# Sums of squares for RMS norms: elementwise adds replaced by matmuls with a block of ones

## The chip, the cores and the metric

One core of a Trainium2 chip runs the whole program. The metric is device time in microseconds; before the change the median of three runs is 2202.68 us (2202.24 to 2213.45). TensorE does the matmuls, VectorE, ScalarE and GpSimd the elementwise work, and SyncE issues the DMAs.

## The reference

Two layers (shared shapes, own weights) run over 128 context tokens and 512 latent tokens, with a model width of 1024. Each layer has a mixer (two kinds of attention and two kinds of state-space scan, concatenated to 1024 features) and a gated convolutional FFN of inner width 2816. Around both stand RMS norms, and these are what the change is about:

```python
def rmsnorm(x, g):
    xf = x.astype(F32)
    y = xf * lax.rsqrt(jnp.mean(xf * xf, axis=-1, keepdims=True) + EPS)
    return (y * g.astype(F32)).astype(x.dtype)

# in each layer
    h = rmsnorm(x, P['g_pre1']) * (1.0 + scale1) + shift1        # then the mixer on h
    y = concat(ya, yb, yc, yd) @ P['w_out']
    x = x + gate1 * rmsnorm(y, P['g_post1'])
    h = rmsnorm(x, P['g_pre2']) * (1.0 + scale2) + shift2        # then the FFN on h
    x = x + gate2 * rmsnorm((jax.nn.silu(g) * v) @ P['w_down'], P['g_post2'])
```

So after each projection two sums of squares over 1024 features are needed per token: one of the projection's output `y`, then one of the new residual `x`, for the next block's norm.

## The kernel before

**Layout.** Features lie on the 128 partitions, in 8 chunks; tokens lie along the free dimension, 642 columns (512 latent, 2 empty, 128 context). The columns are worked in two halves, `SPANS`: 0 to 256 and 256 to 642 (386 columns), called `gi` 0 and 1. Linear layers split each float32 operand into a high and a low part in fp32r and take three products (`lin3`, L116), so that a chunk of 128 x 128 weights costs three matmuls a half.

**A norm.** A sum over features is a sum over 8 chunks and over 128 partitions. `sums` (L297) gives a PSUM tile and a dictionary; `square` (L301) squares a chunk on ScalarE (L309) and adds it to one of two running tiles, even chunks on VectorE and odd ones on GpSimd (L320), then merges the two (L322, L317). `rstd` (L324) sums over partitions: a matmul with 128 tokens of the running tile as weights and one column of ones, 2 token blocks in the first half, 3 in the second, there over two tiles (the eighth chunk's square is left apart). `spread` (L335) scales it and adds EPS on VectorE (L292), raises it to the power -0.5 on GpSimd (L294) and broadcasts it over the partitions by a matmul with the identity. `postnorm` (L381) multiplies `y` by it (L391, VectorE), adds it to `x` (L394, VectorE for even, GpSimd for odd chunks) and squares the new `x`; `prenorm` (L361) makes the next block's input `h` (L371 to L379).

**Buffers.** The first two squares of a sum have tiles of their own (`na00`, `na01`, `na10`, `na11`); all others come from the ring `nsr`, two buffers.

**Order.** Engines work their queues in order. The order in a queue is planned when the program is built, by a planner that simulates the engines and takes ready instructions by priority, which is mostly the order of the code; `prio` sets another. After attention, `run` (L1635 to L1642) goes: output projection of the first half with a square of each chunk (`put`), `norms` of the first half (its residual squares), then the projection of the second half. The prenorm of the first half is held as `pending` and called by `between` when the seventh projection chunk of the second half (`MID` = 6) is issued. The norms of the second half follow, and `ffn_first` starts the FFN's first eight up-projection tiles, of the first half, while these run. After the FFN of layer 0 the same `norms` runs beside the last down-projection (L1453 to L1466), and the first input projections of layer 1 start.

**At the start.** `rstd_first` (L346) already sums the squares of the input in another way: the square of chunk c is the moving operand of a matmul whose weights are 32 columns of ones, into partitions 32 (c mod 4) to +32 of one PSUM tile, two chunks into each. A ScalarE copy brings the tile to SBUF, and a matmul with `sel4` (ones in partitions 0, 32, 64, 96) adds the four rows. There the ring `nsr` has four buffers.

Of the kernel before, what the change touches and what calls it, by code (L numbers as in the profile page):

```python
# [8 lines left out]
F32 = mybir.dt.float32  # L9
F32R = mybir.dt.float32r  # L10
I32 = mybir.dt.int32
AF = mybir.ActivationFunctionType
# [3 lines left out]
P = 128  # L16
# [56 lines left out]
class K:  # L73
# [220 lines left out]
        self.nc.gpsimd.tensor_tensor(y, x, self.c("mhalf")[:, 0:n], op=ALU.pow)  # L294
        return y

    def sums(self, bank):  # L297

        return self.pss(bank), {}

    def square(self, pool, st, gi, src, c, n=8, tmp=None):  # L301


        t0, t1 = SPANS[gi]
        nc = self.nc
        first = n == 8 and c < 2
        tmp = (f"na{gi}{c}", t1 - t0, 1) if first else tmp or NTMP[gi]
        sq = pool.tile([P, tmp[1]], F32, tag=tmp[0], name="nsq", bufs=tmp[2])[:, :t1 - t0]
        nc.scalar.activation(sq, src[:, t0:t1], AF.Square)  # L309
        if first or n < 8:  # L310
            st[1][c] = sq
            return
        if c == 7:
            if gi == 1:
                st[1][c] = sq
            else:
                nc.vector.tensor_add(st[1][0], st[1][0], sq)  # L317
            return
        a = st[1][c % 2]
        (nc.gpsimd if c % 2 else nc.vector).tensor_add(a, a, sq)  # L320
        if c == 6:
            nc.vector.tensor_add(a, a, st[1].pop(1))  # L322

    def rstd(self, pool, st, gi, feats, tag="n"):  # L324

        t0, t1 = SPANS[gi]
        ps, sq = st[0], list(st[1].values())
        n = len(LOC[gi])
        for j, c in enumerate(LOC[gi]):
            for i, t in enumerate(sq):  # L330
                self.mm(ps[:, 400 + j:401 + j], t[:, c - t0:c - t0 + 128], self.c("ones")[:, 0:1], i == 0,
                        i == len(sq) - 1)
        return self.spread(pool, ps, gi, feats, tag)
# [11 lines left out]

    def rstd_first(self, pool, gi, bank):  # L346

        t0, t1 = SPANS[gi]
        ps = self.pss(bank)
        for c in range(8):  # L350
            sq = pool.tile([P, TW - SPLIT], F32, tag="nsr", name="nsq", bufs=4)[:, :t1 - t0]
            self.nc.scalar.activation(sq, self.x[c][:, t0:t1], AF.Square)
            j = c % 4
            self.mm(ps[32 * j:32 * j + 32, 0:t1 - t0], self.c("ones")[:, 0:32], sq, c < 4, c >= 4)
        sb = pool.tile([P, TW - SPLIT], F32, tag="nsr", name="nsb", bufs=4)
        self.nc.scalar.copy(sb[:, 0:t1 - t0], ps[:, 0:t1 - t0])
        for j, c in enumerate(LOC[gi]):
            self.mm(ps[:, 400 + j:401 + j], sb[:, c - t0:c - t0 + 128], self.c("sel4"), True, True)
        return self.spread(pool, ps, gi, 1024, "n")

    def prenorm(self, pool, l, which, gi, r):  # L361

# [38 lines left out]
    def norms(self, pool, gi, st, y, post, pre, out=None):  # L401


        nacc = self.sums("ud"[gi])
        if gi == 1:
            self.between(MID)
        self.postnorm(pool, *post, gi, st, y, None if pre is None else nacc, out)
        if gi == 1 and pre is not None:
            self.prenorm(pool, *pre, 1, self.rstd(pool, nacc, 1, 1024))
        if gi == 0 and pre is not None:  # L410
            self.pending = lambda: self.prenorm(pool, *pre, 0, self.rstd(pool, nacc, 0, 1024))
# [1186 lines left out]
    def run(self):  # L1598
# [3 lines left out]
        with self.pool("cp") as self.cp, self.pool("modp", bufs=2) as self.modp, \  # L1602
# [12 lines left out]
            for l in range(L):  # L1615
                base = 1000000 * l
                with ExitStack() as self.right:
                    with self.pool(f"pm{l}", space=PS) as self.psm:

                        def fill(i, p):  # L1620
                            if l == 0:
                                with self.prio(p):
                                    self.weave(self.adaln(0, 1 + i, 2 + i, self.wp))
                        yp, y = self.mixer(l, base + 100000, fill)
                        for c in range(8):
                            self.dbg(f"yc{l}{c}", self.h[c][0].bitcast(F32))
                        xp = self.right.enter_context(self.pool(f"x{l}", "right"))
                        fp = self.right.enter_context(self.pool(f"f{l}"))
                        with self.prio(base + PR["norm"]):
                            with self.prio(base + PR["wg"]):  # L1630
                                ws = self.w_out_load(l, 2, 1) + self.w_out_load(l, 3, 1)
                            self.x = [xp.tile([P, TW], F32, tag=f"x{c}", name="x") for c in range(8)]
                            for c in range(8):
                                nc.sync.dma_start(self.x[c], xd[:, c, :])
                            for gi, (t0, t1) in enumerate(SPANS):  # L1635
                                st = self.sums("vd"[gi])

                                def put(m):
                                    self.square(fp, st, gi, y[m], m)
                                with self.prio(base + PR["wg"] + 1000) if gi == 0 else ExitStack():  # L1640
                                    self.w_out(l, y, ws, ((t0, t1),), put, WB)
                                self.norms(fp, gi, st, y, (l, 0), (l, 1))  # L1642
                        with self.prio(base + PR["first"]):
                            first = self.ffn_first(l, fp, yp)
                    self.dbg(f"xm{l}", self.x[0])
                    last = l == L - 1
                    xt = o["yT"] if last else self.dp.tile([P, 8, TW], F32, tag="xd", name="xd")
                    with self.prio(base + 320000), self.pool(f"qb{l}", bufs=2, space=PS) as self.pbig:

                        def tables():  # L1650
                            if not last:
                                with self.pool(f"t{l + 1}", "right") as tp, self.prio(base + 320300):
                                    self.s5_tables(l + 1, tp, "dd", base + 320300)
                                self.vec = self.vecs[l]

                        def finish(gi, st, y):
                            self.norms(fp, gi, st, y, (l, 1), None if last else (l + 1, 0), xt)
                        side = ExitStack()
                        wm = None if last else side.enter_context(self.pool(f"wm{l}", "right"))

                        def other():
                            if not last:
                                yield from self.adaln(l + 1, 0, 3, wm, "vu", 3)
                        self.ffn(l, fp, yp, first, tables, finish, other(), side.close)
                    xd = xt
# [145 lines left out]
```

## Time and profile before

| | |
|---|---|
| median of 3 runs | 2202.68 us |
| profiled execution | 2191.5 us, its span 2189.7 us |
| TensorE busy | 1956.1 us, 89% |
| VectorE busy | 1245.6 us, 57% |
| ScalarE busy | 802.4 us, 37% |
| GpSimd busy | 676.4 us, 31% |

The profile is of one execution. In its rows PE is TensorE's matmuls, PEld its weight loads, DVE is VectorE, ACT ScalarE, POOL GpSimd. Times are microseconds from the start of the span unless a column says ns. L81 is the helper through which nearly all matmuls go, so matmuls are told apart by the tiles that they write and read: `nsq` is a square, `nsb` the copy of the start, `rq_y` the reciprocal root, `psp` and `pse` the projection's PSUM tiles. A matmul in fp32 leaves two records (two passes), one in fp32r a single one.

### The profile page before, as it was taken

To read this page: it belongs to the slowest core of one execution; us is meant where nothing else is said; L and a number is where in the kernel's file an instruction comes from. 1 tells how busy PE (TensorE), PEld (TensorE's weight loads), DVE (VectorE), ACT (ScalarE), POOL (GpSimd) and SP (SyncE) were. 2 spreads that over 40 slices of the span, in tenths; PEclk is the share of its full clock that TensorE was granted. 3 is DMA by queue.
4 is the path that set the end of the run, shared out by engine and by line. 5 is a ranking of instruction groups with operands and counts; after the bars stand their busy time and mean duration, and the time that the engine had idled before them with its cause. 6 is when DMAs were issued, how large, how long until landed. Compare 5 with 4: busy or idle time off the path is not lost.

```text
span 2189.7 us, 33260 instructions
## 1 busy us (share of the span) xinstructions
PE 1956.1 (89%) x12812; PEld 1786.6 (82%) x12812; DVE 1245.6 (57%) x2879; ACT 802.4 (37%) x1614; POOL 676.4 (31%) x723
## 2 busy tenths in 40 slices
PE   5996789999699999999988797897985999999997
PEld 2895775876597888999988786876875999999996
DVE  6876785475768575233366475653847631323345
ACT  3423353443452223232343244442444533313241
POOL 3553424200433352122244232323104332212232
PEclk9997789888799999999988887886866999999998
DMA  7464325134305665222224521310112012222221
GB/s 295 136 207 160 114 74 177 40 101 131 107 20 185 197 223 190 85 77 73 91 79 149 184 98 61 117 45 10 51 40 95 20 56 80 73 82 70 75 87 49
DMA packets 93511, 230.29 MB, mean 105 GB/s; under 512 B 17960, under 2 KB 30888, under 8 KB 93352
## 3 DMA queue, kind: packets, MB, share of 16 engines
q1 hardware_dynamic: 82856, 213.46, 29.8%
q10 hardware_dynamic: 10496, 14.71, 1.9%
q8 instruction: 101, 1.65, 0.3%
q14 instruction: 58, 0.48, 0.1%
HBM read 192.21 MB, written 35.92 MB: 104 GB/s over the span
## 4 chain that ended last, share of the span: by engine, by line
PE 67%; DVE 15%; DMA 9%; ACT 3%; issue 2%; POOL 2%; SPq 1%; ACTq 0%; POOLq 0%; DVEq 0%
PE psb L81 34%; PE psp L81 12%; PE psd L81 7%; PE pse L81 6%; PE psv L81 5%; DMA s_tb<-s5td 2%; DMA wm<-in_w_mod 1%; DVE nt L391 1%; PE psu L1209 1%; DMA wr<-in_w_down 1%; DVE x L394 1%; DMA ck<-in_cache_ak 1%; DVE wl L98 1%; DMA q<-d_bq 1%; DVE at_s L1279 1%
## 5 line engine op out<-in xcount | busy, mean ns | idle before, releaser
L81 PE MATMUL psb<-hh,wh 128*128 128x256 f32 (+1 forms) x1152 | 359.1, 312 | 2.3 <-DVE cv L451 2.3
L81 PE MATMUL psb<-hl,wh 128*128 128x256 f32 (+1 forms) x1152 | 358.3, 311 | 0.0
L81 PE MATMUL psb<-hh,wl 128*128 128x256 f32 (+1 forms) x1152 | 357.3, 310 | 0.0
L98 POOL TENSOR_TENSOR wl<-wr,wh 128x1024 fp32r<-128x1024 f32 (+3 forms) x87 | 192.3, 2211 | 502.7 <-ACT wh L95 451.6
L95 ACT CAST wh<-wr 128x1024 fp32r<-128x1024 f32 (+3 forms) x174 | 168.6, 970 | 417.9 <-PE psb L81 283.4
L81 PEld LDWEIGHTS psb<-hh,wh 128*128 128x128 f32 x1152 | 217.9, 189 | 13.3 <-issue 8.2
L81 PE MATMUL psp<-hh,wh 128*128 128x386 f32 (+1 forms) x640 | 215.3, 337 | 10.7 <-ACT hh L374 7.8
L81 PEld LDWEIGHTS psb<-hl,wh 128*128 128x128 f32 x1152 | 218.7, 190 | 3.4 <-issue 3.4
L81 PEld LDWEIGHTS psb<-hh,wl 128*128 128x128 f32 x1152 | 218.1, 189 | 3.4 <-issue 3.4
L81 PE MATMUL psp<-hl,wh 128*128 128x386 f32 (+1 forms) x640 | 209.8, 328 | 0.1
L81 PE MATMUL psp<-hh,wl 128*128 128x386 f32 (+1 forms) x640 | 207.0, 324 | 0.3 <-POOL wl L98 0.3
L98 DVE TENSOR_TENSOR wl<-wr,wh 128x1024 fp32r<-128x1024 f32 (+3 forms) x87 | 100.1, 1151 | 144.0 <-ACT wh L95 143.6
L81 PE MATMUL psb<-uh,wh 128*128 128x256 f32 (+1 forms) x544 | 169.9, 312 | 0.0
L81 PE MATMUL psb<-ul,wh 128*128 128x256 f32 (+1 forms) x544 | 169.4, 311 | 0.0
L81 PE MATMUL psb<-uh,wl 128*128 128x256 f32 (+1 forms) x544 | 169.1, 311 | 0.0
L81 PE MATMUL pse<-k,q 96*128 96x128 f32 (+5 forms) x288 | 107.1, 436 | 44.6 <-ACT at_p L1195 15.1
L81 PEld LDWEIGHTS psp<-hh,wh 128*128 128x128 f32 x640 | 129.0, 202 | 17.4 <-ACT hh L374 8.8
L81 PEld LDWEIGHTS psp<-hl,wh 128*128 128x128 f32 x640 | 129.3, 202 | 2.6 <-issue 1.1
L81 PEld LDWEIGHTS psp<-hh,wl 128*128 128x128 f32 x640 | 128.6, 201 | 1.4 <-issue 0.5
L1419 POOL TENSOR_TENSOR cv<-cv,cv 128x642 f32<-128x642 f32 x44 | 71.6, 1629 | 170.5 <-DVE cv L451 141.2
L81 PEld LDWEIGHTS pse<-k,q 96*128 96x128 f32 (+2 forms) x288 | 60.5, 229 | 77.7 <-issue 32.5
L450 DVE SCALAR_TENSOR_TENSOR cv<-psb,vec,cv 128x641 f32<-128x641 f32 x72 | 63.5, 881 | 103.2 <-ACT cv L449 103.2
(525 smaller groups left out, 4741.7 us busy)
## 6 DMA issues: line engine op xcount, KB each, us to landing
wm<-in_w_mod SPq DMA_DIRECT2D x96, 512.0 KB
wr<-in_w_up SPq DMA_DIRECT2D x88, 512.0 KB
wr<-in_w_in SPq DMA_DIRECT2D x30, 512.0 KB
wr<-in_w_down SPq DMA_DIRECT2D x32, 384.0 KB
wr<-in_w_down SPq DMA_DIRECT2D x32, 320.0 KB
wr<-in_w_out SPq DMA_DIRECT2D x16, 512.0 KB
s_tb<-s5td SPq DMA_DIRECT2D x8, 992.0 KB
s_to<-s5td SPq DMA_DIRECT2D x8, 768.0 KB
```

Of the source, the lines that this page charges most:

```text
L81: self.nc.tensor.matmul(out, w, x, start=start, stop=stop)
L95: nc.scalar.copy(hv, rv)
L98: e.tensor_sub(lv, rv, hv.bitcast(F32))
L391: nc.vector.scalar_tensor_tensor(t, y[c][:, t0:t1], gg[:, c, g:g + 1], r(t0, t1), op0=ALU.mult, op1=ALU.mult)
L394: (nc.gpsimd if c % 2 else nc.vector).tensor_add(xs, xs, t)
L450: nc.vector.scalar_tensor_tensor(out[:, 1:TW], x[:, 0:TW - 1], w[:, 0:1], out[:, 1:TW], op0=ALU.mult, op1=ALU.add)
L1209: nc.tensor.transpose(ps[:, 128 * j:128 * j + 128], s, self.c("ident"))
L1279: V.reduce_max(s[:, k:k + 1], ps, axis=AX.X)
L1419: G.tensor_mul(cv[0], cv[0], cv[1])
```

## The change

`sums` gets a flag. With it the sum is done as at the start: each square is made in `nsr`, goes to TensorE as the moving operand against 32 columns of ones, and `rstd_pe` copies and finishes. The flag is set for the squares of the output projection (`run`), for the residual squares in `norms` (after the output projection in both layers and after the FFN of layer 0), and at the start, where `rstd_first` now calls the shared functions and thereby has two `nsr` buffers, not four. The squares of the FFN's output keep the elementwise way, and `ssd`'s norm too.

```diff
-    def sums(self, bank):
-        return self.pss(bank), {}
+    def sums(self, bank, pe=False):
+        return self.pss(bank), None if pe else {}
+
+    def square_pe(self, pool, ps, gi, src, c):
+        t0, t1 = SPANS[gi]
+        sq = pool.tile([P, TW - SPLIT], F32, tag="nsr", name="nsq", bufs=NTMP[gi][2])[:, :t1 - t0]
+        self.nc.scalar.activation(sq, src[:, t0:t1], AF.Square)
+        j = c % 4
+        self.mm(ps[32 * j:32 * j + 32, 0:t1 - t0], self.c("ones")[:, 0:32], sq, c < 4, c >= 4)
+
+    def rstd_pe(self, pool, ps, gi):
+        t0, t1 = SPANS[gi]
+        sb = pool.tile([P, TW - SPLIT], F32, tag="nsr", name="nsb", bufs=NTMP[gi][2])
+        self.nc.scalar.copy(sb[:, 0:t1 - t0], ps[:, 0:t1 - t0])
+        for j, c in enumerate(LOC[gi]):
+            self.mm(ps[:, 400 + j:401 + j], sb[:, c - t0:c - t0 + 128], self.c("sel4"), True, True)
+        return self.spread(pool, ps, gi, 1024, "n")
 
     def square(self, pool, st, gi, src, c, n=8, tmp=None):
+        if st[1] is None:
+            return self.square_pe(pool, st[0], gi, src, c)
...
     def rstd(self, pool, st, gi, feats, tag="n"):
+        if st[1] is None:
+            return self.rstd_pe(pool, st[0], gi)
...
     def rstd_first(self, pool, gi, bank):
-        t0, t1 = SPANS[gi]
-        ps = self.pss(bank)
+        st = self.sums(bank, True)
         for c in range(8):
...
+            self.square(pool, st, gi, self.x[c], c)
+        return self.rstd(pool, st, gi, 1024)
...
     def norms(self, pool, gi, st, y, post, pre, out=None):
-        nacc = self.sums("ud"[gi])
+        nacc = self.sums("ud"[gi], True)
...
                             for gi, (t0, t1) in enumerate(SPANS):
-                                st = self.sums("vd"[gi])
+                                st = self.sums("vd"[gi], True)
```

## Rows read from the trace of the kernel before

**Rows 1.** The page: busy time of each engine; chain that ended last, by engine.
```profile
PE 1956.1 (89%) x12812; PEld 1786.6 (82%) x12812; DVE 1245.6 (57%) x2879; ACT 802.4 (37%) x1614; POOL 676.4 (31%) x723
PE 67%; DVE 15%; DMA 9%; ACT 3%; issue 2%; POOL 2%; SPq 1%; ACTq 0%; POOLq 0%; DVEq 0%
```

**Rows 2.** Windows after attention, layer 0: length, busy by engine, granted clock, DMA.
```profile
555.58:567.45 11.87, 11.87 (x77) 11.87 (x78) 8.31 (x20) 4.63 (x11) 2.34 (x3) 1.00 0.13 46
568.00:590.00 22.00, 2.26 (x9) 1.86 (x8) 20.52 (x33) 11.97 (x23) 14.68 (x11) 0.55 0.38 136
590.00:597.00 7.00, 6.75 (x30) 6.46 (x31) 6.36 (x11) 5.46 (x13) 4.79 (x4) 0.50 0.31 105
597.00:621.50 24.50, 23.88 (x200) 23.49 (x199) 15.91 (x37) 5.89 (x15) 10.06 (x14) 0.99 0.06 21
```

**Rows 3.** Waits of TensorE, whole span: releaser, total us, times, longest.
```profile
PE psu L81 <- DVE nsq L317: 27.2, 2, 13.6
```

**Rows 4.** The tile nsq: count, ns min/median/max, first and last start, shapes.
```profile
L320 DVE TENSOR_TENSOR nsq<-nsq x42: 409/556/2471, 556.9 to 2169.7; 128x256 f32<-128x256 f32 x21, 128x386 f32<-128x386 f32 x21
L320 POOL TENSOR_TENSOR nsq<-nsq x28: 722/964/1611, 557.0 to 2169.4; 128x256 f32<-128x256 f32 x14, 128x386 f32<-128x386 f32 x14
L81 PE MATMUL psu<-nsq,cst x16: 487/488/513, 22.0 to 26.0; 128*32 128x386 f32 x16
```

**Rows 5.** Timeline of TensorE: start, us; second-half reductions, new form and old.
```profile
27.42 0.83 PE L81 MATMUL psu<-cst,nsb 128*128 128x1 f32 x6
...
614.43 1.50 PE L81 MATMUL psd<-cst,nsq 128*128 128x1 f32 x12 [0.62 <-DVE nsq L322]
```

**Rows 6.** Timeline of ScalarE, the start.
```profile
26.55 0.48 ACT L356 COPY nsb<-psu 128x386 f32<-128x386 f32 x1 [1.80 <-PE psp L81]
```

**Rows 7.** Timeline of TensorE, the start: two squares at once, two passes.
```profile
25.66 0.50 PE L81 MATMUL psu<-nsq,cst 128*32 128x386 f32 x2
...
25.98 0.50 PE L81 MATMUL psu<-nsq,cst 128*32 128x386 f32 x2
```

**Rows 8.** Timeline of TensorE, the start: full-width and 32-wide matmuls in turn.
```profile
46.59 0.38 PE L81 MATMUL pse<-hl,wh 128*128 128x256 f32 x1
46.81 0.28 PE L81 MATMUL pse<-hh,wl 128*128 128x256 f32 x1
...
47.52 0.28 PE L81 MATMUL pse<-hh,wl 128*128 128x256 f32 x1
47.73 0.64 PE L81 MATMUL psp<-wm,sc 128*32 128x512 f32 x4
```

**Rows 9.** Timeline of TensorE, layer 0, from the projection's end.
```profile
567.45 0.60 PE L81 MATMUL psv<-identr,rq_y 128*128 128x128 f32 x4
581.66 0.98 PE L81 MATMUL psu<-cst,nsq 128*128 128x1 f32 x4 [13.61 <-DVE nsq L317]
...
590.15 0.58 PE L81 MATMUL psp<-hh,wh 128*128 128x256 f32 x1 [3.48 <-ACT hh L374]
...
591.48 2.72 PE L81 MATMUL psd<-cst,nsq 128*128 128x1 f32 x12
```

**Rows 10.** Timeline of GpSimd: the first half's reciprocal root.
```profile
564.73 0.71 POOL L294 TENSOR_TENSOR rq_y<-rq_x,cst 128x2 f32<-128x2 f32 x1 [5.52 <-DVE rq_x L292]
```

**Rows 11.** Timeline of ScalarE: last residual squares, then the third of the second half.
```profile
578.95 0.72 ACT L309 ACTIVATE nsq<-x 128x256 f32<-128x256 f32 x2 [1.65 <-DVE nsq L320]
580.49 0.53 ACT L309 ACTIVATE nsq<-y 128x386 f32<-128x386 f32 x1 [0.82 <-DVE nsq L320]
```

**Rows 12.** Timeline of VectorE: that square's input; the first scaling of the prenorm.
```profile
561.90 0.56 DVE L1567 TENSOR_TENSOR y<-y,psp 128x386 f32<-128x386 f32 x1 [0.24 <-PE psp L81]
...
588.12 1.64 DVE L371 SCALAR_TENSOR_TENSOR nt<-x,gpre,psu 128x256 f32<-128x256 f32 x4
```

**Rows 13.** Timeline of TensorE, layer 0 after the FFN: its two reductions.
```profile
1140.21 0.59 PE L81 MATMUL psd<-cst,nsq 128*128 128x1 f32 x2 [2.02 <-DVE nsq L322]
...
1161.91 2.72 PE L81 MATMUL psd<-cst,nsq 128*128 128x1 f32 x12 [4.47 <-DVE nsq L322]
```

More of the change, by code (lines that the diff above doesn't have):

```diff
@@ L346, in rstd_first @@
     def rstd_first(self, pool, gi, bank):
-        t0, t1 = SPANS[gi]
-        ps = self.pss(bank)
+        st = self.sums(bank, True)
         for c in range(8):
[L351 to L359, printed above, removed]
+            self.square(pool, st, gi, self.x[c], c)
+        return self.rstd(pool, st, gi, 1024)
     def prenorm(self, pool, l, which, gi, r):
```

## The prediction

> **What bounds the kernel now.** I read the engine totals and the chain that ended last first: TensorE is busy for 89% of the span and is 67% of the chain, VectorE 57% and 15% [rows 1]. So on average an elementwise add is cheap and a matmul is dear, but the change sits in five short stages, and each has its own limit. I therefore took windows around one of them (layer 0, after attention) [rows 2]. From 555.58 to 567.45 us, the output projection, TensorE has no gap: 11.87 of 11.87 us. From 568 to 590 it works for 2.26 us while VectorE works for 20.52 of 22. From 590 on it is full again, at half rate up to 597 (granted clock 0.50, the 1.2 GHz level) and then at the full 2.4 GHz. The list of TensorE's waits shows the price of the middle stretch: two waits of 13.6 us on the last add of squares, one a layer [rows 3]. Layer 1 repeats the pattern (1652 to 1716 us); the third place is layer 0 after the FFN.
>
> **What goes.** Ten of the fourteen sums of squares change (the four of the FFN's output stay). With three VectorE and two GpSimd chunk adds a sum, 30 of the 42 and 20 of the 28 adds go; at the medians 0.556 and 0.964 us [rows 4] that is 16.7 us of VectorE and 19.3 us of GpSimd, besides the adds that merge. None of it counts by itself, only what of it lay on the path of its stage. The 80 ScalarE squares stay. Each second-half reduction shrinks: twelve matmul records over two sources (1.50 us at full rate) become six over one (0.83 us) [rows 5], behind a new ScalarE copy of 0.48 us [rows 6].
>
> **What comes: 80 matmuls of 32 weights, in fp32.** The start of the kernel already does this. A pass over 386 columns is 0.488 us long [rows 4], and the second pass starts 0.32 us after the first (25.66 and 25.98) [rows 7]. A square of 386 columns therefore holds TensorE 0.64 us at full rate, one of 256 columns 0.42 (scaled by columns, an estimate). Two that stand side by side share the array: 25.66 to 26.48, 0.82 us for two [rows 7]. Placed in a stream of full-width matmuls there is a toll at either end: 47.52 to 47.73 is 0.21 us and 46.59 to 46.81 is 0.22, where the step between such matmuls is 0.12 (256 columns, 0.28 long with overlap) [rows 8]. So 0.19 us for each lone square. The Trainium skill ("TensorEngine Tiling (Array Packing)", Key Properties) says that a change of tiling mode drains the engine, which speaks against scattering such squares; these rows agree with a toll but change the number format too, and without any toll T1 below would be at most 3.4 instead of 4.9.
>
> **T1, first-half squares of the output projection (two layers).** The stage is TensorE-bound, so 8 x (0.42 + 0.19) = 4.9 us if the broadcast of the reciprocal root (567.45) stays behind all projection matmuls. But the root itself was ready at 564.73 + 0.71 = 565.44 [rows 9, 10], 2.0 us earlier; the planner may put it ahead of the last matmuls now. Bounds: -0.5 (the merging adds gone, broadcast moved) and +4.9. I take 4.9 - 2.0 = +3.0.
>
> **T2, the VectorE-bound stretch to the first FFN matmul (two layers).** Before: the last residual square ends at 579.67 (two from 578.95) [rows 11], TensorE sums the columns at 581.66 [rows 9], and the first scaling is at 588.12 [rows 12]: 8.45 us. The adds leave this tail, and about 0.7 us of adds and their slowing of VectorE goes ahead of it. What replaces them is a queue: all squares now share one ring of two buffers, also the copy that the reduction needs. Buffers go out in program order: the second-half square at 580.49 had its input since 561.90 + 0.56 = 562.46 [rows 12], and came only behind all residual squares [rows 11]. In the new order the copy for the first half is asked for after seven second-half squares (the seventh projection chunk calls the pending norm). So seven squares must pass first, by pairs: ScalarE 0.53 [rows 11], TensorE 0.64 at full or 1.29 at half rate, 0.2 assumed for signals: 1.37 or 2.02 us a pair. The first starts 0.6 after the last residual square, the seventh three pairs later. Full rate: seventh done at 0.6 + 4.1 + 1.3 = 6.0, column sums 0.5 (half of 0.98), root 0.71 and signals 1.0, broadcast 0.6 [rows 9, 10], scaling at 8.2. Half rate: 0.6 + 6.1 + 1.9 = 8.6, then 0.98, 1.0, 1.2, and 12.0 with a signal. Against 8.45 and with the 0.7: -0.95 or +2.85. Behind it, TensorE did 2.72 us of sums and 4.4 us of half-rate matmuls from 590.15 to 597.3 [rows 2, 9]; at full rate that is 0.75 with 0.64 for the eighth square, and 2.2, a gain of 3.5; at half rate about 0. Bounds -4.5 and +2.8. The engine is idle from 568.05 before the level falls and works nearly without gap for 7 us before it rises [rows 2, 9]; the new squares fill the end of that idle stretch, so I expect the rise within them: -1.0, near the middle. The Trainium skill ("TensorE: Matmul & The Clock Gate", HAM oscillation) says that idle gaps throttle the engine and steady activity frees it; if the squares from 572 us on count as such activity, T2 is the lower bound, -4.5, which is part of the second rival below.
>
> **T3, residual squares of the second half (two layers).** TensorE is full from 597 to 621.5, 23.88 of 24.5 [rows 2], with FFN matmuls that do not need this norm, so all is paid. ScalarE makes the squares mostly by twos. Side by side 4 x (0.82 + 0.19) = 4.0, singly 8 x 0.83 = 6.6; less 0.67 for the smaller reduction [rows 5]: +3.3 to +6.0. The old 0.62 us wait for the last add [rows 5] may go as well: +2.9. I take 4.4.
>
> **T4, waits inside the stream (two layers).** TensorE takes its queue in order, and 16 instructions a layer in full streams now wait for a ScalarE square; behind each stand matmuls that were ready. The nearest row is the one such wait of before, 0.62 us [rows 5]; 0 to 4 us, I take 0.5, since the old sums were issued 2 us and more after their inputs.
>
> **T5, layer 0 after the FFN.** First-half residual squares add up to 4.9 us to a full down-projection stream, but TensorE idles 2.02 us at its end; the second-half ones lie before an idle stretch of 4.47 us that ends with 2.72 us of half-rate sums [rows 13]. There half of the 2.72 goes, with two adds of 0.56 just ahead and some 0.9 of adds earlier; a last square at half rate (1.29) and the copy (0.48) come: -1.6. Together -1 (-3 to +4). **T6, the start:** its squares drop from four buffers to two and ScalarE may stand behind a square; the weights that gate the first norm come later anyway: +0.5 (0 to 2.5).
>
> **Sum.** Two layers x (3.0 - 1.0 + 4.4 + 0.5) = 13.8, with T5 and T6 13.3 us. The profiled execution took 2191.5 us (span 2189.7); it would be 2204.8, or 1.0061 times. It was 11 us below the median of the runs shown, 2202.68 (2202.24 to 2213.45), so on that scale 2216 us. Below, times are on that scale, and 0.5%, 11 us, is about what a measurement of this kernel can tell from no change.
>
> **Rivals.** *Forecast*, matmul work on the bound engine: +5 to +21, 2208 to 2224; chance 0.45. *Faster*: the ring does not hold the first-half reduction back and the clock stays up. Then the tail of T2 is 0.54 (square) + 0.48 (copy) + 0.6 + 1.0 + 0.6 = 3.2 instead of 8.45; with the 0.7 and the 3.5 that is -9.4; T1 0, T3 +2.9: -6.5 a layer, T5 -3, in all -16, 2187. For it: 13.6 us waits on an add; against it: the order of squares in [rows 11]. It decides at the copy: if it runs right behind the eighth residual square, this holds. Chance 0.12. *Worse*: half rate all through T2 and in-order stalls: 4.9 + 2.8 + 6.0 + 2.0 a layer, T5 and T6 near their upper ends: +37; half of that beyond the forecast is likelier, near 2233. For it: granted clock 0.55 there; chance 0.18. *No effect*: squares fall into gaps and the VectorE relief pays for the rest, T1 0 and T2 -3: 2198 to 2207. For it: VectorE-bound stretch; against it: no gap in the streams. Chance 0.25. That the adds would not go can be excluded: ten calls change their branch.
>
> **From cases to numbers.** Faster by over 0.5%: most of the second case, 0.10. Slower: two thirds of the forecast (0.30) and all of the worse case (0.18), 0.48. Within: 0.42. The range 2196 to 2234 leaves out 0.1 below and some 0.08 above.
>
> **What would show it.** Right: the projection stage longer by 2 to 5 us with eight 32-wide matmuls in it; the first-half copy behind seven second-half squares; first FFN matmul within 3 us of its old distance but at full clock sooner; 4 to 5 us more TensorE in the next 25 us. Wrong: the copy directly behind the residual squares, squares that cost much under 0.5 us each in a stream, or a program whose later order shifted by more than these terms.

## The result

The changed kernel takes 2255.28 us (median of four runs, 2253.39 to 2256.17) against 2202.56 us for the kernel before on the same chip: ratio 1.0251, 95% interval 1.0221 to 1.0282. It is slower by 53 us where I forecast 13, and above the end of my range. The direction was right, the size was not.

The page of the kernel after (busy time by engine), to be read beside [rows 1]:

```profile
PE 2006.6 (89%) x12942; PEld 1787.0 (79%) x12942; DVE 1210.4 (54%) x2834; ACT 808.9 (36%) x1624; POOL 654.6 (29%) x703
```

The change did what it says: VectorE works 35 us less, GpSimd 22 us less, TensorE 50 us more.

**Where the 63 us are.** The span of the profiled execution grew from 2189.7 to 2252.7 us. I took the same instruction in both traces and noted by how much it starts later; the shift changes in few places. Boundaries: the first 256-column addition from `pse` to y in the last pass of a layer's output projection, points within the two FFNs (700, 1090 and 1780 us of the kernel before, each the median shift of TensorE's instructions within 4 us), and 1190 us, where the second layer's mixer has begun. The table gives the change in each stretch against the kernel before (first line: its own lengths), in us, for one profiled execution of every kernel; the stretches inside the FFNs, within 2.1 us everywhere, are left out. Ratios are of runs on one chip, with their 95% intervals.

| kernel | median, before beside it | ratio | start, mixer 0 | projection 0 | end of FFN 0 | mixer 1 | projection 1 |
|---|---|---|---|---|---|---|---|
| before | | | 555.4 | 144.6 | 100.0 | 462.3 | 127.7 |
| after | 2255.3, 2202.6 | 1.0251 (1.0221 to 1.0282) | +9.7 | +12.8 | +13.3 | +7.8 | +20.3 |
| again | 2256.9, 2196.6 | one run | +8.0 | +14.3 | +12.1 | +10.7 | +20.5 |
| pework | 2253.1, 2197.6 | 1.0248 (1.0231 to 1.0265) | +12.6 | +14.0 | +3.3 | +20.1 | +18.9 |
| pegroup | 2230.4, 2192.3 | 1.0182 (1.0159 to 1.0205) | -3.7 | +13.1 | +4.6 | +4.0 | +15.6 |
| tiny | 2214.1, 2192.6 | 1.0096 (1.0067 to 1.0124) | +1.9 | +4.3 | +2.6 | +3.0 | +7.6 |
| ring4 | 2242.6, 2197.6 | 1.0203 (1.0188 to 1.0218) | +3.2 | +11.4 | +3.0 | +20.3 | +13.2 |
| copyout | 2233.6, 2192.3 | 1.0196 (1.0152 to 1.0239) | -3.8 | +8.9 | +9.3 | -0.2 | +16.4 |
| onlyx | 2226.8, 2197.6 | 1.0137 (1.0114 to 1.0159) | +12.9 | +7.5 | +14.6 | +2.1 | +9.1 |
| onlyy | 2230.8, 2197.6 | 1.0142 (1.0119 to 1.0165) | +2.1 | +3.5 | +0.2 | +16.2 | +10.3 |
| l1all | 2212.2, 2192.6 | 1.0072 (1.0051 to 1.0093) | +1.4 | +0.3 | +1.2 | -4.2 | +19.3 |
| l1f | 2232.6, 2192.3 | 1.0190 (1.0161 to 1.0219) | +6.4 | -2.1 | +10.1 | +19.7 | +8.0 |
| l1x0 | 2193.8, 2192.6 | 0.9996 (0.9978 to 1.0013) | +2.0 | -0.1 | 0.0 | +1.5 | +1.3 |
| start2 | 2220.8, 2196.6 | 1.0123 (1.0080 to 1.0166) | +4.7 | +0.1 | -0.2 | +24.3 | +2.1 |
| ctrl | 2231.8, 2196.6 | 1.0165 (1.0127 to 1.0204) | +5.4 | 0.0 | +11.0 | +26.6 | 0.0 |
| allf4 | 2203.4, 2192.3 | 1.0060 (1.0038 to 1.0081) | +7.5 | -7.3 | +8.7 | +7.5 | +1.5 |
| allf5 | 2196.9, 2196.6 | 1.0009 (0.9985 to 1.0033) | +10.9 | -6.1 | -2.1 | -0.1 | +1.1 |

So of the 63 us, 33 are in the two projections with their norms, 13 around the end of layer 0's FFN, and 17 in stretches in which the change edits at most two buffers.

**Layer 0 after attention.** Windows of the kernel after (length; busy PE, PEld, DVE, ACT, POOL; granted clock; DMA), from the first addition to y to the broadcast of the first half's root, from there to the first FFN matmul, and on from it; compare [rows 2]:

```profile
565.14:585.25 20.11, 16.50 (x93) 12.66 (x93) 8.52 (x18) 5.41 (x11) 3.18 (x2) 1.00 0.15 52
585.25:610.76 25.51, 16.65 (x56) 6.66 (x57) 12.67 (x25) 14.95 (x30) 9.54 (x8) 0.63 0.45 145
610.76:640.00 29.24, 29.24 (x194) 23.15 (x194) 13.11 (x36) 9.62 (x21) 9.04 (x13) 0.97 0.00 1
```

The broadcast comes 20.11 us after the first addition (before: 12.01). TensorE has idle time in this stretch, 3.6 us, where it had none. The middle stretch is VectorE-bound no more (12.67 of 25.51 busy, before 20.52 of 22) and not shorter for it. The timeline of TensorE in the same place (start, duration) shows one lone square:

```profile
566.68 0.28 PE L81 MATMUL pse<-hh,wl 128*128 128x256 f32 x1
566.89 0.62 PE L81 MATMUL psv<-nsq,cst 128*32 128x256 f32 x2
567.44 0.39 PE L81 MATMUL psp<-hh,wh 128*128 128x256 f32 x1
567.66 0.28 PE L81 MATMUL psp<-hl,wh 128*128 128x256 f32 x1
```

From 566.68 to 567.66 are 0.98 us in which two full-width steps of 0.12 (from start to start) were done: 0.74 us for one square of 256 columns. My estimate was 0.61. Two squares side by side cost 0.75 together (four records from 576.60, between steps of the stream).

### The profile page after: what moved, and what is told of

Read it like the earlier page. It is cut to its first block, busy times and chain, and to the rows that moved or that the text cites. A ratio compares the mean times of both kernels' runs of the same rounds, so it can differ in the third digit from the quotient of the medians.

```text
span 2252.7 us, 33483 instructions
## 1 busy us (share of the span) xinstructions
PE 2006.6 (89%) x12942; PEld 1787.0 (79%) x12942; DVE 1210.4 (54%) x2834; ACT 808.9 (36%) x1624; POOL 654.6 (29%) x703
## 4 chain that ended last, share of the span: by engine, by line
PE 67%; DVE 12%; DMA 10%; issue 5%; ACT 3%; POOL 2%; SPq 1%; ACTq 0%; POOLq 0%; DVEq 0%
PE psb L81 34%; PE psp L81 13%; PE psd L81 7%; PE pse L81 6%; PE psv L81 4%; DMA wm<-in_w_mod 1%; DMA s_tb<-s5td 1%; DMA k<-d_ak 1%; DMA wr<-in_w_down 1%; PE psu L1222 1%; DVE at_s L1292 1%; DMA q<-d_bq 1%; DMA d_ak<-qk_lo 1%; PE psu L81 1%; DVE wl L98 1%
## 5 line engine op out<-in xcount | busy, mean ns | idle before, releaser
L81 PE MATMUL psp<-hh,wh 128*128 128x386 f32 (+1 forms) x640 | 218.9, 343 | 13.3 <-ACT hh L387 6.0
```

The lines of the kernel that those rows point to most:

```text
L81: self.nc.tensor.matmul(out, w, x, start=start, stop=stop)
```

## Experiments

Two theories at first. **B**: the new matmuls cost by themselves, because TensorE is full where they stand. **A**: they cost by hand-over, since each square needs one of two buffers and a place in TensorE's in-order queue before the buffer is free again. A third, **C**, came with the results: any edit gives the whole program another plan (order and memory), and the unchanged stretches feel it.

### pework: the matmuls without the ring

```diff
+    (kernel before, in square:)
+        if len(st) > 2:
+            self.mm(st[0][32 * j:32 * j + 32, 0:a1 - a0], self.c("ones")[:, 0:32], src[:, a0:a1], c < 4, c >= 4)
```

> The kernel before with all its elementwise squares, adds and buffers, and besides them the 80 matmuls of the change (ones of 32 columns by the unsquared chunk, into the same PSUM tile at the same places of the program; their sums are used by nothing). TensorE has all the new work, but no matmul waits for a square and no buffer of squares waits for a matmul. Theory A (the change costs by its hand-overs: a square must get a place in TensorE's queue before its one of two buffers comes free): the matmul work alone is a small part, 8 x 0.6 us a sum in two sums of each layer at most, so +10 to +20 us, 2212 to 2222. Theory B (TensorE is the bound, and its added matmuls and the tolls around them are the cost): nearly all of the +52, 2240 to 2255.

The projections lost 14.0 and 18.9 us, as much as in the kernel after (12.8 and 20.3), though every elementwise add was still there and no matmul waited for a buffer of squares. So in both stages the matmuls alone are enough for the loss, as theory B says; what dropping the adds saves must have been taken back by something (ring4 below). At the end of layer 0's FFN only +3.3 came: the +13.3 there is not matmul work. The total, equal to that of the whole change, is a coincidence of two different sums: 32.9 of it in the projections, 32.7 in mixers where nothing was changed.

### ring4 and copyout: the buffers

```diff
+        tag, n, bufs = (f"na{gi}{j}", t1 - t0, 1) if j < 2 else NTMP[gi]      (ring4)
-        sb = pool.tile([P, TW - SPLIT], F32, tag="nsr", name="nsb", bufs=NTMP[gi][2])
+        sb = pool.tile([P, t1 - t0], F32, tag=f"na{gi}0", name="nsb", bufs=1)  (ring4, copyout)
```

> The kernel after, with every square still summed by TensorE, but the squares of each sum in four buffers instead of two (chunks 0, 1, 4, 5 take tiles that the dropped adds leave idle), and the copy of the sums in such a tile too, so that it is queued behind no square of the other half. Theory A: the 1 to 4 us waits of ScalarE for TensorE and the 7.6 us wait of TensorE for the copy mostly go; with the matmul work left the time is 2212 to 2228. Theory B: the matmuls are the same 80, so 2245 to 2258. A third possibility: the waits only move, since the planner puts each matmul behind its square into the stream whatever the buffers; then 2235 to 2250, with the projection stream as long as in the kernel after (15.9 us).

> The kernel after with one edit: the ScalarE copy of the sums goes to a tile of its own, not into the ring of two, so that it no longer stands behind seven squares of the other half; the squares keep their two buffers. If the place of the copy in the ring was the price of the 113 us stretch around the end of layer 0's FFN (TensorE waited 7.6 us for a copy there), that stretch falls from +13.3 to +3, as with four buffers, and the time from the first scaling to the first prenorm from 22.3 and 24.5 us to 19 to 21: 2238 to 2246. If it was the squares' own two buffers (three waits of ScalarE of 3 to 4 us for TensorE there), nothing changes: 2252 to 2258. The projection stream keeps its 20.1 and 21.5 us to the broadcast either way.

Four buffers take the end of layer 0's FFN from +13.3 to +3.0, the matmul work that pework shows there; the copy's own tile alone takes it to +9.3, between its two expectations (+3, or no change). So 10 of those 13 us are theory A, about 4 of them the copy's place in the ring and 6 the squares' two buffers. The waits of ScalarE around that place (total us, times, longest), first the kernel after, then ring4:

```profile
ACT nsq L306 <- PE psu L81: 11.3, 4, 3.9
```

```profile
ACT nsq L308 <- PE psu L81: 2.1, 1, 2.1
```

(In ring4 the squares of the FFN's output, L329, wait another 4.4 us for TensorE.)

TensorE in the kernel after pays for it in one wait for the copy, which stood behind the second-half squares of the FFN's output:

```profile
1173.25 1.01 PE L81 MATMUL psu<-cst,nsb 128*128 128x1 f32 x4 [7.57 <-ACT nsb L313]
```

In the projections four buffers gave 1.4 and 7.1 us, far from all: the streams stay full. Beside pework, which has the same 80 matmuls and all the adds, ring4 lost 2.6 and 5.7 us less there. As an estimate from one execution of each, that is what dropping the adds is worth, and the ring of two takes most of it back. ring4's expectation of 2212 to 2228 by theory A was missed (its ratio makes 2247 of 2202.6), and its total decides little, since 20.3 us of it came in mixer 1. The copy's own tile came out at the 2238 to 2246 of its expectation only by the ratio (1.0196 of 2202.6 is 2246).

### tiny and pegroup: columns or change of shape

```diff
-            self.mm(st[0][32 * j:32 * j + 32, 0:a1 - a0], self.c("ones")[:, 0:32], src[:, a0:a1], c < 4, c >= 4)
+            self.mm(st[0][32 * j:32 * j + 32, 0:4], self.c("ones")[:, 0:32], src[:, a0:a0 + 4], c < 4, c >= 4)   (tiny)
+            st[2].append(src)          (pegroup; rstd issues the eight of a sum in a row)
```

> As the kernel that keeps all of before and adds the 80 matmuls, but these read 4 columns of the chunk each instead of 256 or 386: their number, their places in the program and their waits stay, their column time goes. Their sums are used by nothing. Theory B with the columns as the price: the projection stages lose +2 to +5 each instead of +14 and +19 (what is left is the toll of a 32-column matmul in a stream). If the toll is the price and not the columns: +8 and more each. Theory C: the mixers change their order all the same and lose some +5 to +20 in each layer though nothing is done in them, so the whole is +10 to +35; without theory C the whole is +4 to +12.

> As the kernel that keeps all of before and adds the 80 matmuls, but the eight matmuls of a sum stand side by side, just ahead of its column sums, instead of one by one behind their chunks; their columns and number are the same, and their sums are used by nothing. If the price of a lone square is the change of TensorE between full-width and 32-column matmuls (8 lone 4-column matmuls lengthened the projection stream by 4.0 us, 8 of 256 columns by 8.1): the stream grows by 2 to 4 us instead of 8.6 to 9.8, and the second-half sums cost about 4 instead of 7, so the projection stages lose +6 to +9 each instead of +14 and +19, the whole 2220 to 2232. If columns alone are the price: nearly as before the regrouping, +12 to +17 a stage, 2240 to 2253.

The stages lost 4.3 and 7.6, the second more than expected; the runs of tiny spread widely (2197.9 to 2226.9), so its total says little. With four columns each, twelve lone matmuls (eight of the first half, four of the second) stood ahead of the first broadcast and made the way to it 4.0 us longer (16.03 for 12.01): 0.34 us apiece with almost no columns. This is tiny's timeline:

```profile
558.32 0.28 PE L81 MATMUL psp<-hh,wl 128*128 128x256 f32 x1
558.52 0.23 PE L81 MATMUL psv<-y,cst 128*32 128x4 f32 x2
558.68 0.39 PE L81 MATMUL pse<-hh,wh 128*128 128x256 f32 x1
558.91 0.28 PE L81 MATMUL pse<-hl,wh 128*128 128x256 f32 x1
```

From 558.32 to 558.91 is 0.59 where two steps of 0.12 stand: 0.35 us. So of a lone square's 0.74 us about half has nothing to do with columns: 0.08 ahead of the square and 0.11 behind it, together the 0.19 that I had read from [rows 8], and 0.16 from the square to the next matmul. The other 0.39 are its 256 columns in fp32, over three times the 0.12 of such a matmul in fp32r. The Trainium skill ("TensorEngine Tiling (Array Packing)", Key Properties) says that a change of tiling mode drains the engine; these rows fit that, with the 0.19 us at the two ends. But the number format changes there too: in the stream of the kernel before, two full-width fp32 matmuls of one column each (563.82) cost 0.43 us together, 563.65 to 564.44 less two steps of 0.18, with nothing lost ahead of them and 0.08 behind. How much of a square's 0.35 is the shape alone was not separated; the version that would have told it, 32-wide squares in fp32r, one pass, has no result. pegroup was the miss: the planner did not keep the eight of a sum together (in layer 0 they start at 552.8, 554.3, 555.7, 557.2, 557.2, 559.0, 560.8 and 562.6, with full-width matmuls between), so issuing them in a row in the code gave little, and it tells nothing more on the toll.

### onlyx, onlyy, l1all, l1x0: one part at a time

```diff
-                                st = self.sums("vd"[gi], True)
+                                st = self.sums("vd"[gi])             (onlyx; onlyy: the same in norms)
+        nacc = self.sums("ud"[gi], post == (1, 0))                   (l1all; run: l == 1; start as before)
+        nacc = self.sums("ud"[gi], post == (1, 0) and gi == 0)       (l1x0; run: none; buffers as ring4)
```

> The kernel after, but the squares of the output projection are added elementwise again; only the sums of the residual (and of the start) go to TensorE. By stages of the trace of the kernel after, the output projection with its norm gives back +8 of the +13 to +20 us a layer, the sums of the residual in the FFN stream (+7 a layer) and after the FFN of layer 0 (+13) stay: 2225 to 2238 by theory A. By theory B half of the matmuls in full streams go: 2228. If the copy is queued early because no square of the output projection shares the ring, the stretch up to the first FFN matmul is shorter than in either kernel, and it could be 2215.

> The kernel after, but the squares of the residual are added elementwise again; only those of the output projection (and of the start) go to TensorE. By stages the projection keeps its +8 us a layer, the FFN stream loses its +7 a layer, and the +13 around the end of layer 0 goes: 2218 to 2230 by both theories; the sum of the excesses of this kernel and of the one with only the residual on TensorE should be the +52 of the whole change (plus the start's, which both have) if the two parts do not meddle with each other, and less if the shared ring of two buffers makes them wait for each other (theory A).

> The change in layer 1 alone: only the four sums of squares after the attention of layer 1 go to TensorE (32 matmuls of squares), the start and all of layer 0 are as before. TensorE's queue is the same as before, instruction for instruction, until the first of these squares, so mixers, layer 0 and the start can't differ. Theory B (matmul work on the bound engine, paid where it stands; the runs with the matmuls as pure extra lost 14.0 us in this stage in layer 0 and 18.9 in layer 1): +14 to +20 in the output projection and norms of layer 1, nothing elsewhere: 2212 to 2218. Theory C (much of the loss is the order in which the planner puts the unchanged mixers, whose time grew by 2 to 20 us in every changed kernel): the same here, but then the change of two layers would be only about twice this, +30 to +40 of +52, with the rest in the mixers. Theory A (the ring of two buffers): also +14 to +20; it does not decide here.

> Only one sum on TensorE: the residual of the first half in layer 1, in four buffers (two of them tiles that the dropped adds leave idle) with the copy of the sums in such a tile too. It stands in the stretch in which TensorE is idle for 13.6 us and waits for the last add of this sum, so its eight matmuls cost nothing, and the adds and their queue go. If the add was the bound of that stretch: 3 to 6 us faster, 2197 to 2200 on the scale of 2202.7. If VectorE's other work (scaling, adding to the residual) is the bound of it: the same, within 2 us. If the squares still wait for buffers behind those of the second half: slower by 2 to 4 us.

In the projections the two halves add up: 7.5 and 3.5 in layer 0 (12.8 together in the kernel after), 9.1 and 10.3 in layer 1 (20.3). So there they hardly meddle with each other (the sums fall short by 1.8 and 0.9 us, where two executions of the kernel after differ by 1.5). The end of layer 0's FFN belongs to the residual squares alone (+14.6 and +0.2). l1all is the clean test, since TensorE's queue is the same, instruction for instruction, up to the first square in layer 1: +19.3 in that stage and 1.0072 in all. By that ratio it is 16 us for one layer, more than my sum for the whole kernel. onlyy's ratio makes 2234 of 2202.7, above the 2230 of its expectation; 16.2 us of it came in mixer 1.

l1x0 shows what became of the idle 13.6 us [rows 3]. The first scaling to first prenorm took 17.73 instead of 21.89 us, and the first FFN matmul came 1.55 us sooner still after it; but from there to the steady FFN it took 96.58 instead of 90.35. The gain was given back in full. This is TensorE's longest wait there (total, times, longest), for chunks of h:

```profile
PE psp L81 <- ACT hh L396: 6.0, 2, 4.6
```

and this is its window at the start of that FFN, with 3.49 of 5 us busy and at half rate:

```profile
1688.00:1693.00 5.00, 3.49 (x14) 3.20 (x15) 5.00 (x6) 3.19 (x7) 3.54 (x3) 0.50 0.35 122
```

Here an earlier norm only started the FFN on chunks that were not normed yet.

### ctrl, start2, again: what an edit costs that computes nothing

```diff
+            self.onesr = self.cp.tile([P, 128], F32R, tag="onr", name="onesr")
+            nc.vector.tensor_copy(self.onesr, self.c("ones")[:, 0:1].to_broadcast([P, 128]))   (ctrl)
-            sq = pool.tile([P, TW - SPLIT], F32, tag="nsr", name="nsq", bufs=4)[:, :t1 - t0]
+            sq = pool.tile([P, TW - SPLIT], F32, tag="nsr", name="nsq", bufs=2)[:, :t1 - t0]   (start2)
```

> The kernel before with one tile of 512 bytes a partition more, written once at the start (a VectorE copy) and used by nothing. All sums are elementwise as before. Theory C (the plan of the whole program, order and memory, moves with any edit, and mixers and the end of layer 0's FFN are the places that feel it): the stage around the end of layer 0's FFN +10 (TensorE waits 11.5 us there for the cast of a weight tile, as in the two kernels with such a tile), the mixer of layer 1 +10 to +20, projections +-2; in all 2215 to 2232 on the scale of 2202.7, though nothing in the computation changes. Without theory C: 2200 to 2206.

> The kernel before with the two buffers at the start that the change brings in place of four, and nothing else. If the start's buffers are the cause of the +3.6 of the first 140 us: +3 to +4 there, and the rest as before, 2205 to 2208. With theory C besides: the order of the mixers moves too, +5 to +20 more, 2208 to 2225. If the start's weights hide it: 2200 to 2205.

> A second execution of the kernel after, unchanged, for the spread of its stages. The projection stages within 1 us of +12.8 and +20.3, the end of layer 0's FFN within 1 us of +13.3; the mixers, with their DMAs, may differ by up to 10 us from +9.7 (start and mixer of layer 0) and +7.8 (mixer of layer 1). If the projection stages too move by more than 3 us, the split by stage says little.

A tile that nothing reads costs 1.65%, and the start's two buffers alone 1.23%, half of the whole change's ratio; on the scale of 2202.7 that is 2239 and 2230, above the upper ends of both expectations (2232 and 2225). The start's two buffers are part of the change, and its weights do not hide them. In ctrl both projections are within 0.05 us of before, so the table can be trusted there; the loss is in mixer 1 and at the end of layer 0's FFN. Windows of mixer 1, before and ctrl:

```profile
1190.00:1652.30 462.30, 394.33 (x2403) 353.97 (x2403) 274.01 (x678) 180.18 (x454) 116.96 (x134) 0.79 0.26 84
```

```profile
1206.50:1695.40 488.90, 403.02 (x2434) 361.22 (x2433) 272.46 (x681) 179.95 (x455) 118.44 (x139) 0.78 0.25 79
```

VectorE and ScalarE do the same work; TensorE idles 18 us more, and 9 us more of its work falls into this window (part of it are matmuls on a weight tile of the FFN that stand ahead of the boundary in the kernel before, so the split between +11.0 and +26.6 is rough by that much). What makes it idle was not found. Its longest wait in that mixer, at a transposition in the attention, is 6.4 us before, 13.8 in ctrl and 14.0 in the kernel after; but allf5 waits 14.8 us there, and its mixer 1 is as long as before.

At the end of layer 0's FFN, ctrl's +11.0 is a wait for the cast of a weight tile:

```profile
PE psp L81 <- ACT kh L95: 11.5, 1, 11.5
```

The kernel after has nothing of this wait, so its own +13.3 there is the ring and the matmul work, as ring4 says. Whether order or memory does it in ctrl was not separated.

How much of such a shift is one execution's chance? The second execution of the kernel after (again) repeated the projection stages within 1.5 us, the end of layer 0's FFN within 1.2, both a little over the 1 us expected, and the mixers within 2.9. Up to the first projection TensorE's queue in pework, pegroup, tiny, l1all and l1x0 is that of before, and in onlyx, onlyy and (but for five records) start2 that of the kernel after. With the queue of before, start and mixer 0 took -3.7 to +12.6; with that of after, +2.1 (onlyy), +4.7, +8.0, +9.7 and +12.9 (onlyx). So for start and mixer 0 theory C is not shown: the after's +9.7 is within the spread of the same queue, except some 3 us in the first 140, which start2 repeats (+3.0; pework, with the start of before, has +1.8 there).

In mixer 1, two kernels with the queue of before (l1all, l1x0) took -4.2 and +1.5; the others, ctrl and start2 among them, have other queues and took -0.2 to +26.6. So theory C is shown there for ctrl and start2, whose ratios, over four runs each, stand behind the traces. Another queue need not cost anything, though (copyout -0.2, allf5 -0.1), and that the after's own +7.8 (again +10.7) comes from its queue is likely, not shown.

### l1f, allf4, allf5: the same sums at full width

```diff
-        self.mm(ps[32 * j:32 * j + 32, 0:t1 - t0], self.c("ones")[:, 0:32], sq, c < 4, c >= 4)
+        self.mm(ps[:, 0:t1 - t0], self.onesr, sq, c == 0, c == 7)     (sq and onesr in fp32r; allf4, allf5: four buffers)
```

> As the kernel with the change in layer 1 alone (+19.3 in its stage, 2212 where before had 2193), but the squares are written in fp32r and summed against 128 columns of ones in fp32r: one pass instead of two, and the same full-width shape as the matmuls around them. The sums, now the same in all 128 partitions, are a little less exact; ring, copy and places in the queue stay. Theory B in the sharpened form (price is two fp32 passes plus the change of shape): a 256-column pass costs 0.12 us in the stream, a 386-column one 0.18, so the projection stream grows by 1 to 1.5 us instead of 9.6 and the FFN stream by about 1.5 instead of 7: +3 to +6 in the stage. Theory A (waiting for hand-overs): +12 and more, since every square still has to pass its two buffers and the queue.

> A candidate for a better version: the sums of the output projection and of the residual in both layers on TensorE, squares in fp32r against 128 columns of ones in one pass, four buffers a sum (two in tiles that the dropped adds leave idle), the copy in such a tile, and the start as before. The projection streams lose about 1 us each, the FFN streams 1.5, the stretch around the end of layer 0's FFN 0 to 2; the first-half adds and their tail go, worth 0 to 4 a layer (the kernel with only that sum on TensorE got its first scaling to prenorm 4.2 us sooner and gave it back in the FFN). In all -6 to +6 beside the mixers' own spread of some 5: 2190 to 2210 on the scale of 2202.7. By theory A it is slower than 2215.

> The candidate with fp32r squares against 128 columns of ones and four buffers, with the ones held in the place of the constant that they replace, so that no memory is added. If the extra tile was the cause of the 11.5 us wait for a weight cast: the stretch around the end of layer 0's FFN falls from +8.7 to 0 or below, the projection of layer 0 stays at -7 and that of layer 1 near +1; 2190 to 2200 on the scale of 2202.7, so the same as before or slightly faster. If the plan of the mixers costs again: 2200 to 2212.

One fp32r pass against 128 columns of ones needs no change of shape. In l1f's stream such a square takes one step of 0.12 us, with nothing lost ahead of it or behind:

```profile
1689.31 0.28 PE L81 MATMUL psv<-nsq,onesr 128*128 128x256 f32 x1
1689.43 0.28 PE L81 MATMUL psp<-hh,wh 128*128 128x256 f32 x1
```

With the ring of two (l1f), projection 1 lost 8.0 instead of 19.3; 6.3 of it was the way to the broadcast, where the squares' matmuls came in pairs some 3.5 us apart, held by the ring (ScalarE waits 8.5 us for its buffers there); so the stage lies between its two expectations. Its losses before that stage are ctrl's, whose queue it shares up to there. allf4 has ctrl's tile too, and the same 11.5 us wait at the end of layer 0's FFN, and its ratio makes 2216 of 2202.7, above the 2210 of its expectation; allf5 holds the ones in the place of an older constant, and the wait and the +8.7 are gone. With four buffers besides (allf5) it lost 1.1, and projection 0 gained 6.1. So both prices are real: the form of the matmul (shape and number format together), and behind it the ring. allf5 as a whole is 1.0009 of before (0.9985 to 1.0033): the same. Its stages gained 7.1 us in that execution; start and mixer 0, +10.9, took them back. No version tried beats the kernel before.

## Why the prediction was wrong, step by step

Three terms of the sum failed: the place of the broadcast in T1, the size of T3, and T5, which gave the ring no price. Beside them the unchanged stretches, which the sum put at nothing, lost 17 us.

**T1** (+3.0 a layer): measured +8.1 and +9.4 (broadcast after 20.11 and 21.48 instead of 12.01 and 12.05). The matmul part, 4.9, was about right: a lone square costs 0.74 us where I had 0.61, but four of the eight stood in pairs, and TensorE's busy time in the stretch grew by 4.6 (16.50 for 11.87). The missing 0.13 of a lone square is not at its ends but in its own hold: 0.55 us (566.89 to 567.44), where I had scaled 0.42 out of [rows 7], between whose two passes other 32-wide matmuls run (25.87). What failed is the place of the broadcast. I took off 2.0 us because it might move ahead; it moved behind instead, and left 3.6 us of idle time. Before, the column sums stood 8.4 us into the stretch, with projection matmuls to hide the root; now the last squares end the stream, and copy, sums, root and broadcast follow it in the open:

```profile
582.25 0.61 PE L81 MATMUL psv<-cst,nsb 128*128 128x1 f32 x4 [1.09 <-ACT nsb L313]
585.25 1.23 PE L81 MATMUL psv<-identr,rq_y 128*128 128x128 f32 x4 [2.38 <-POOL rq_y L294]
```

Layer 1 has the same two waits (1.09 and 2.53 us), and 1.3 us more because part of the stretch ran at half rate (granted clock 0.90 for 1.00). ScalarE waited 6.1 us for buffers in the stream of layer 0, four times; but with four buffers (ring4) the broadcast came after 19.89 us, hardly sooner.

**T2 to T4** (+3.9 a layer together): +4.7 in layer 0, +10.8 in layer 1. The copy behind seven squares, the queue and the place of the first FFN matmul came as T2 had them at half rate (+2.8 and +2.4 to that matmul, for +2.85). T3 was too small: the second-half squares do not stand side by side, each of the eight stands alone, in both layers:

```profile
618.48 0.28 PE L81 MATMUL pse<-hl,wh 128*128 128x256 f32 x1
618.69 0.84 PE L81 MATMUL psd<-nsq,cst 128*32 128x386 f32 x2
619.46 0.39 PE L81 MATMUL pse<-hh,wl 128*128 128x256 f32 x1
619.68 0.28 PE L81 MATMUL psp<-hh,ul 128*128 128x256 f32 x1
```

From 618.48 to 619.68, less two steps of 0.12, is 0.96 us a square; eight of them, less the 0.67 of the smaller reduction, are 7.0, above T3's upper bound of 6.0. T4 came to nothing: no matmul of these streams waited for a square (29.24 of 29.24 us busy in layer 0). That layer 0 came out near the sum is luck: behind the first FFN matmul it lost only 1.9 us, because it had its full clock back within 3 us of that matmul instead of 7 (granted clock 0.74 from 611 to 614, then 1.00) and the old sums of 2.72 us no longer stood there. T2 had counted both, and they hid most of the 7.0. In layer 1 neither was to be had: the kernel before did these sums ahead of the first FFN matmul (1687.07, that matmul 1689.65) and had a short half-rate stretch behind it (granted clock 0.50 from 1689 to 1692, then 0.82 and 1.00), the kernel after a longer one (0.50 from 1745 to 1748, then 0.80 and 1.00). So the 7.0 came undiminished and 1.5 with it: +8.5. I had worked out one layer and doubled it.

**T5** (-1): +13.3. The step counted matmul work and gave no price to the ring there, though I had seen the ring as a queue in T2. pework prices the work at +3.3, ring4 at +3.0; the other 10 us are the ring and the copy's place in it.

**T6** (+0.5): the first 140 us lost 3.6, and start2 3.0, so the start's weights did not hide the two buffers, though T6 assumed it. The larger miss is beside it: 17 us in start and mixers, of which I said only, as a thing that would make me wrong, that the later order could shift by more than these terms. By the ratios of start2 and ctrl an edit that adds no work to the sums can cost 27 to 36 us in this kernel, two to three times my whole sum. How much of the 17 is the change's plan and how much one execution's chance stays open.

Adding up what was missed: T1 5.1 and 6.4, T2 to T4 0.8 and 6.9, T5 14.3, start and mixers 17.0, less 0.7 in the FFNs, are 49.8, and with 13.3 the 63.1 us measured.

**The rivals.** Worse had the full streams right, but not the size; its in-order stalls came at the end of layer 0's FFN (7.57 us in one wait), not in the streams. Faster named a mechanism that exists: l1x0's tail is 4.2 us shorter. In layer 1 it was worth nothing, for the FFN behind it is fed by the same norm. In layer 0 it was worth something once the squares were cheap and had four buffers: projection 0 was 7.3 and 6.1 us shorter in allf4 and allf5, in one execution of each.

## What to carry to other kernels

A reduction moved to a full TensorE is paid per matmul as well as per column if its form differs from its neighbours' (here 0.35 us of 0.74 had nothing to do with columns): take the price from a lone one in a stream of the same two forms, or keep the full width and one pass. Ask what hides the rest of the chain (copy, sums, root, broadcast) once the stream it stood in has become longer. Count every buffer ring through which the moved work must pass, at every place where it is used, and not only where you first see it queue. And where a planner orders the whole program, run a control that computes nothing new (an unused tile), and the same kernel twice, before a per cent or two is credited to, or blamed on, a change.

## What the hardware showed that I had not expected

With the queue of the kernel before, TensorE's granted clock can fall in one execution and stay up in another. Windows in mixer 0, before and pework (whose queue is the same up to 568 us):

```profile
490.00:500.00 10.00, 10.00 (x51) 4.98 (x47) 3.90 (x9) 2.69 (x7) 0.00 (x0) 1.00 0.51 161
```

```profile
492.00:502.00 10.00, 10.00 (x28) 4.52 (x27) 4.02 (x13) 1.40 (x5) 0.00 (x0) 0.60 0.41 114
```

TensorE was busy without a gap in both; in pework the clock fell to 0.50, the 1.2 GHz level, within the window, in before it stayed at 1.00, the 2.4 GHz level. pework got through 28 matmul records at 0.60 where before had 51 at 1.00, and was 10 us late from there on. Its profiled run took 2262.0 us, its three others 2251.7 to 2253.3. A shift of that size in one trace is no effect of an edit until a second execution shows it.
